# Two second products moved into an attention's opening steps, its first two normalisations moved to another engine, four output rows stored plainly

## The chip, the cores and the metric

The kernel runs on one core of a Trainium2 chip. A core has TensorE (PE, matmuls; its weight loads are listed as PEld), VectorE (DVE), ScalarE (ACT), GpSimd (POOL) and SyncE (SP, which here only issues DMAs). The metric is the device time of one execution in microseconds (us); lower is better.

## The reference

One layer of an encoder block: an input projection of the normalised stream feeds a retention branch and a windowed attention branch; both are gated, projected, mixed by sigmoid gates, projected once more, normalised, and added to x. T is 1040 (16 meta tokens and 1024 positions), the model width 1024.

```python
u = _rms_norm(h, pre_w)
z = u @ w_in
rq, rk, rv, rg, aq, ak, av, ag, gr, ga = _split_in(z)
...
o_r = o_r * ret_nw.astype(jnp.float32) * jax.nn.silu(rg.astype(jnp.float32))
y_r = o_r.astype(h.dtype) @ w_rb
...
s = jnp.concatenate([s_band, s_meta], axis=-1)
m = jnp.maximum(jnp.max(s, axis=-1, keepdims=True), sink_l)
p = jnp.exp(s - m)
p = p / (jnp.sum(p, axis=-1, keepdims=True) + jnp.exp(sink_l - m))
...
o_a = o_a * jax.nn.silu(ag.astype(jnp.float32))
y_a = o_a.astype(h.dtype) @ w_ab
mix = jax.nn.sigmoid(gr) * y_r + jax.nn.sigmoid(ga) * y_a
out = mix @ w_o
return h + _rms_norm(out, post_w)
```

## The kernel before

Every matmul is done in three parts (`mm3`, lines 94 to 96): operands are split into a high and a low part (ACT casts the high part, DVE subtracts it at line 110), and high by high, low by high and high by low are summed in PSUM. The large projections are Strassen-like block products: seven products of half-size blocks, whose operands are sums and differences of weight or stream blocks, made on DVE, and whose results DVE and ACT add into the outputs. A phase is named by a letter, and its products accumulate in tiles `by`, `bz`, `br`, `ba` and `bo`.

The program runs in this order: a setup and the retention heads (to about 335 us), the first phase with tiles `by` (gates and queries), the attention, and then the phases z (gates), r and a (the two branch projections) and o (the output projection).

*Units.* Ten output units (`LATER`, numbers 4 to 15) have three of their seven products done early, as fill between other work: their product 2 ("second products", tiles `pe4_2` to `pe15_2`) and their products 3 and 5 ("fifths", tiles `pe4_5` and so on). A unit's second product is 12 matmuls of 128 x 512, in four pieces of three. In the first phase a table, `FIRST_AT`, says at which step of the program which job is written (an engine may do it earlier or later): `m4` is four pieces of second products, `x0` and `y0.0` load and split parts of the output weight, `L4`, `S4`, `P4` and `F4` belong to the weights of unit 4 for the fifths. The names at line 854 (load `we`), 861 to 863 (its sums, on DVE) and 790 (`w5_...h`, the cast) are these steps.

*Attention.* It goes by 32 steps of 64 queries, 16 for each of two groups of heads. `stage1` makes masked scores for two tiles (`ps` on PE, `raw` with its row minimum `nm` on DVE, line 1525; the exponential `p` with its row sum on ACT, 1528; the reciprocal of the sum on DVE, 1531; p times that reciprocal on POOL, 1538, or for the last blocks of the second group on ACT, 1535). `stage2` transposes p on PE (`pt`, 1549 and 1552) and splits it, `stage3` multiplies it with the values (`po`). Between these, `fill` runs pieces of the fifths: `START` gives the numbers ahead of the first two blocks' scores, `FILL` two numbers for each later step, each in half pieces; `BEGUN` says at which piece the jobs of the fifths (loads, sums, splits) are started. A second product's piece and a fifth's piece are each three matmuls and cost two.

*Output.* `o_post` takes each finished half row block (128 rows of 512). Squares go to ACT, the mean's power to POOL, and the normalised rows are written by POOL with an accumulating DMA to `out`, where x was copied ahead during the retention heads. Row 3 alone loads x into SBUF and is finished by DVE and stored plainly by SP.

The order within each engine is that of the program, with explicit marks (`follow`) that keep DVE and ACT work behind the scores and transposes.

Of the kernel before, what the change touches and what calls it, by code (L numbers as in the profile page):

```python
# [12 lines left out]
D = 1024  # L13
# [10 lines left out]
HALVES = [(16, 528), (528, 1040)]  # L24
MW = 720
NC = 2 * NB
START = 4, 12
FILL = ((2, 2),) * 1 + ((3, 1),) * 1 + ((2, 3),) * 1 + ((2, 2),) * 1 + ((4, 3),) * 1 + ((2, 3),) * 6 + ((2, 4),) * 1 + ((2, 3),) * 1 + ((2, 4),) * 1 + ((2, 3),) * 1 + ((3, 3),) * 1 + ((2, 1),) * 1 + ((2, 2),) * 1 + ((2, 3),) * 2 + ((2, 4),) * 1 + ((0, 4),) * 1 + ((2, 2),) * 1 + ((2, 3),) * 3 + ((3, 3),) * 1 + ((2, 4),) * 1 + ((1, 3),) * 1
EARLY = 8, 9
LATER = 4, 10, 5, 11, 6, 12, 7, 13, 14, 15  # L30
PRE = {u: (2, 3, 5) for u in LATER}
BORDER = 12, 0, 12
LAST = 9
REFILL = -48, 6, 5
LATE = -15, -14, -12, -9, -7, -6, -5, -3, -3, -1

LEADS = 2, 4, 6
VALUES_AT = ((-1, "w1", "s0", "s1"), (1, "l2"), (4, "w0"), (6, "c2"), (8, "n6", "s2", "pT2.0.1.2"),
             (16, "f0", "l3"), (17, "f1", "f2"), (20, "c3", "z"), (21, "s3", "f3"), (22, "pT2.3"))
FIRST_AT = ((1, "k6"), (2, "pT3"), (6, "pT4"), (7, "m4"), (12, "tT3", "tT4"), (13, "x0"), (14, "tT2"),  # L40
# [4 lines left out]

U_QK, U_V, U_G = 0, 4, 8
# [9 lines left out]
def block_kernel(ctx: ExitStack, tc: tile.TileContext, xT, x, meta, w_in, w_rb, w_ab, w_out, vecs, dec, sink,  # L56
# [463 lines left out]
    def retention(h, fill):  # L520
# [127 lines left out]
        def finish(c):  # L648
            o = op[c - 1]
            to = (p2 if c > 2 else p1)(f"to{h}_{c}")  # L650
            for e_ in range(2):
                nc.tensor.transpose(to[:, P * e_:P * e_ + P], o[:, P * e_:P * e_ + P], ident)  # L652
            if c % 2 == 0:
                ost[0] = rp.tile([P, 2, 256], F32, tag="ost", bufs=2, name=f"ost{h}_{c}")
            w0 = P * ((c - 1) % 2)
            for e_ in range(2):
                nc.scalar.activation(ost[0][:, e_, w0:w0 + P], to[:, P * e_:P * e_ + P], AF.Copy,  # L657
                                     scale=rnw[:, 2 * h + e_:2 * h + e_ + 1])
            if c % 2 == 1:
                sent = nc.sync.dma_start(  # L660
                    oTr_d[2 * h:2 * h + 2, :, P * (c - 1):P * (c + 1)].rearrange("e p t -> p e t"), ost[0]).ins
                if h < NH - 1 and c == 5:
                    with tc.issue_after(sent):
                        r, e_ = ((0, 3), (4, 6), (6, 8))[h]
                        nc.sync.dma_start(out[P * r:P * e_], x[P * r:P * e_])

        for c in range(NB, 0, -1):
# [311 lines left out]
    def gtile(name):  # L979
        return gp.tile([P, 512], F32, tag="g", bufs=gates_[0], name=name)  # L980
# [205 lines left out]
    def refill(nm, src):  # L1186
# [38 lines left out]
        def got(n):  # L1225
            return lambda: get_pre(n)
# [34 lines left out]
            return d  # L1261
        if nm == "a":
            return {-16: [load(0, 0)], -14: [load(1, 1)], -13: [plain("B11", 0, 0)], -11: [got("T1")],
                    -10: [load(1, 0)], -9: [got("T2")], -7: [plain("B21", 1, 0)], -5: [got("T3")],
                    -3: [plain("B22", 1, 1)], -1: [got("T4")]}
        return {-16: [load(0, 0), load(0, 1)], -14: [load(1, 1)], -13: [plain("B11", 0, 0)], -11: [t1],
                -10: [load(1, 0)], -9: [t2, t3], -7: [b21], -5: [plain("T3", 0, 1)], -3: [plain("B22", 1, 1)],
# [105 lines left out]


    pw = rbc[:, 0:D]
    rows, xres = {}, []

    def o_head():
        nc.sync.dma_start(pw, post_w.partition_broadcast(P))
# [5 lines left out]
    def o_post(u, i, j, o, to=None):  # L1385
        if not rows:
            o_head()
        r = 2 * (u ^ 2) + i
        s = slice(512 * j, 512 * j + 512)
        if r not in rows:  # L1390
            rows[r] = (gp.tile([P, 3], F32, tag="ms2", bufs=4, name=f"ms2_{r}"), [], [])
            if r == 3:
                xres.append(lp.tile([P, 4, 256], F32, tag="wr", bufs=2, name="xres").rearrange("p a b -> p (a b)"))
                nc.sync.dma_start(xres[0], x[P * r:P * r + P])
        m2, parts, _ = rows[r]
        square(r, m2, j, o)
        to = o if to is None else to
        if u == 3:
            to = gtile(f"pw{r}_{j}")
            nc.vector.tensor_tensor(to, o, pw[:, s], mul)  # L1400
        parts.append((s, to, o))
        if len(parts) == 2:
            o_out(r)

    def square(r, m2, c, o):
        m1 = rows[r][2]
        jk = gtile(f"jk{r}_{c}")
        nc.scalar.activation(jk[:, 0:o.shape[1]], o, AF.Square, accum_out=m2[:, c:c + 1])
        if not m1:
            m1.append(gp.tile([P, 1], F32, tag="ms1", bufs=4, name=f"ms1_{r}"))  # L1410
            nc.vector.tensor_scalar(m1[0], m2[:, c:c + 1], 0.25 / D, EPS, op0=ALU.mult, op1=ALU.add)
        else:
            nc.vector.scalar_tensor_tensor(m1[0], m2[:, c:c + 1], 0.25 / D, m1[0], op0=ALU.mult, op1=ALU.add)

    def o_out(r):
        m2, parts, (m1,) = rows[r]
        nc.gpsimd.tensor_tensor(m1, m1, mhalf[:, 0:1], ALU.pow)
        for s, to, o in parts:
            if r == 3:
                nc.vector.scalar_tensor_tensor(to, to, m1, xres[0][:, s], op0=ALU.mult, op1=ALU.add)  # L1420
                nc.sync.dma_start(out[P * r:P * r + P, s], to)
                continue
            if r == 2:
                nc.scalar.activation(to, to, AF.Copy, scale=m1)
            else:
                nc.vector.scalar_tensor_tensor(to, o, m1, pw[:, s], op0=ALU.mult, op1=ALU.mult)
            nc.gpsimd.dma_start(out[P * r:P * r + P, s], to, accum_op=ALU.add)

    def o_tail(o, a):
        m2, parts, _ = rows[3]  # L1430
        s = slice(a, a + 256)
        square(3, m2, 2 * (a // 256), o[:, s])
        if not a:
            xres.append(gtile("pw3_0"))
        nc.vector.tensor_tensor(xres[1][:, s], o[:, s], pw[:, s], mul)
        if a:
            parts.append((slice(0, 512), xres[1], o))
            o_out(3)

    seq = [(u, p) for p in (1, 7, 5, 6, 2, 3, 4) for u in (0, 1)]  # L1440
# [49 lines left out]
    def attention():  # L1490
# [18 lines left out]
        def stage1(g, b):  # L1509
# [21 lines left out]
            last["sum"] = nc.vector.reciprocal(den, den).ins  # L1531
            softmax.append(last["sum"])
            for e_ in range(2):
                if g and b > 2 * NB - 3:
                    softmax.append(nc.scalar.activation(pt[e_][:, 0:wid], pt[e_][:, 0:wid], AF.Copy,
                                                        scale=den[:, e_:e_ + 1]).ins)
                    continue
                nc.gpsimd.tensor_scalar(pt[e_][:, 0:wid], pt[e_][:, 0:wid], den[:, e_:e_ + 1], 1.0, op0=ALU.mult,  # L1538
                                        op1=ALU.mult)
# [40 lines left out]


        chunks = [(g, b) for g in range(2) for b in range(2 * NB)]
        works = hooked([(fifths(), 2)], BEGUN)
        owed = [0]

        def fill(n):
# [142 lines left out]
    for n, _ in enumerate(first):  # L1729
# [8 lines left out]
    yp = spare[0] = at1  # L1738
    vah, val = (atv.tile([P, NB, 256], R, name=n) for n in ("vah", "val"))

    BEGUN = {5: [(pre_sums, 5), (pre_fetch, 11)],
             6: [(pre_parts, 5)],
             7: [(pre_low, 5)],
             13: [(pre_sums, 11), (pre_fetch, 6)],
             14: [(pre_parts, 11)],
             15: [(pre_low, 11)],
             21: [(pre_sums, 6), (pre_fetch, 12)],
             22: [(pre_parts, 6)],
             23: [(pre_low, 6)],
             24: [(load_k,)],  # L1750
             29: [(pre_sums, 12), (pre_fetch, 7)],
             30: [(pre_parts, 12), (pre_low, 12)],
             37: [(pre_sums, 7), (pre_fetch, 13)],
             38: [(pre_parts, 7)],
             39: [(pre_low, 7)],
             40: [(pre_load, 3, act_src(w_out))],
             45: [(pre_sums, 13), (pre_fetch, 14)],
             46: [(pre_parts, 13)],
             47: [(pre_low, 13)],
             48: [(pre_split, 3, 0)],  # L1760
             50: [(pre_split, 3, 1)],
             52: [(pre_split, 3, 2)],
             53: [(pre_sums, 14), (pre_fetch, 15)],
             54: [(pre_parts, 14), (pre_split, 3, 3)],
             55: [(pre_low, 14)],
             61: [(pre_sums, 15)],
             63: [(pre_parts, 15), (pre_low, 15)]}

    i = attention()
    next(i)  # L1770
# [112 lines left out]
```

## Time and profile before

| what | us |
|---|---|
| runs | 1049.03, 1053.14, 1053.15 (median 1053.14) |
| the profiled execution | 1051.43 |
| its span | 1049.7 |
| PE busy in the span | 1030.0 |
| DVE, ACT, POOL busy | 842.1, 511.0, 217.5 |

The profile's times are those of one execution, of which 1.7 us lie around the span. PE's busy time is that of its matmuls, which overlap: one matmul of 512 columns shows about 0.39 us and is followed by the next after about 0.23. "Waits" tell for which instruction of another engine an engine stood idle.

### The profile page before, as it was taken

How to read it: one execution, taken by the hardware profiler on the slowest of the kernel's cores; microseconds unless marked ns; L12 is line 12 of the kernel's file. 1: busy time of each engine (PE TensorE's matmuls, PEld its weight loads, DVE VectorE, ACT ScalarE, POOL GpSimd, SP SyncE). 2: the span in 40 equal slices, each digit the busy share in tenths (PEclk: the TensorE clock that was granted, in tenths of full speed). 3: DMA queues.
4: the chain of work that ended last, by engine and by line, in shares of the span. 5: the costliest groups of instructions: out<-in, count | busy, mean ns of one | idle time of the engine just before them, and what ended most of it. 6: DMA issues, size and time to landing. Idle time of an engine off the chain costs nothing.

```text
span 1049.7 us, 17233 instructions
## 1 busy us (share of the span) xinstructions
PE 1030.0 (98%) x5797; PEld 893.0 (85%) x5797; DVE 842.1 (80%) x1734; ACT 511.0 (49%) x1116; POOL 217.5 (21%) x284
## 2 busy tenths in 40 slices
PE   8999999999999999999899999999999999999997
PEld 7998999989999888888689998888888888787885
DVE  7887788779889787985878886699899799768665
ACT  5541441423435643423567777476567355343443
POOL 3424235235233002231123321000000000111042
PEclk9999999999999999999899999999999999999998
DMA  9422311315244499997866775999889648789365
GB/s 335 161 81 91 101 42 51 111 32 200 77 141 142 124 409 322 262 312 217 313 213 211 233 246 161 357 374 347 308 300 336 237 138 269 195 237 316 95 101 81
DMA packets 117577, 217.17 MB, mean 207 GB/s; under 512 B 12672, under 2 KB 44320, under 8 KB 114864
## 3 DMA queue, kind: packets, MB, share of 16 engines
q1 hardware_dynamic: 111040, 204.78, 56.9%
q0 software_dynamic: 6304, 11.01, 7.0%
q8 instruction: 46, 0.75, 0.3%
q14 instruction: 43, 0.35, 0.1%
q10 hardware_dynamic: 144, 0.27, 0.1%
HBM read 142.57 MB, written 77.12 MB: 209 GB/s over the span
## 4 chain that ended last, share of the span: by engine, by line
PE 86%; DVE 5%; DMA 5%; issue 1%; SPq 1%; ACT 1%; POOL 0%; DVEq 0%; POOLq 0%; ACTq 0%
PE bz L95 5%; PE bz L94 5%; PE bz L96 5%; PE by L95 4%; PE by L96 4%; PE by L94 4%; PE pv L95 3%; PE pv L94 3%; PE pv L96 3%; PE bo L95 3%; PE bo L94 3%; PE br L95 2%; PE bo L96 2%; PE br L94 2%; PE br L96 2%; PE ba L95 2%
## 5 line engine op out<-in xcount | busy, mean ns | idle before, releaser
L94 PE MATMUL pv<-wh,big 128*128 128x256 f32 x256 | 73.3, 286 | 0.0
L95 PE MATMUL pv<-wh,big 128*128 128x256 f32 x256 | 72.9, 285 | 0.0
L96 PE MATMUL pv<-wl,big 128*128 128x256 f32 x256 | 72.5, 283 | 0.0
L1538 POOL TENSOR_SCALAR p<-p,den 128x352 f32<-128x352 f32 (+2 forms) x60 | 38.4, 653 | 127.2 <-DVE den L1531 109.9
L1369 POOL DMA_DIRECT2D mx_d<-c1a x4 | 3.5, 875 | 287.3 <-DVE c1a L1360 287.3
L94 PE MATMUL bz<-T,lhz 128*128 128x512 f32 x144 | 56.8, 395 | 0.0
L95 PE MATMUL bz<-T,llz 128*128 128x512 f32 x144 | 56.8, 394 | 0.0
L96 PE MATMUL bz<-T,lhz 128*128 128x512 f32 x144 | 56.8, 394 | 0.0
L1012 ACT CAST why<-wry 128x512 fp32r<-128x512 f32 x56 | 33.2, 620 | 48.3 <-PE by L96 27.1
L95 PE MATMUL by<-big,wly 128*128 128x512 f32 x128 | 50.7, 396 | 0.0
L94 PE MATMUL by<-big,why 128*128 128x512 f32 x128 | 50.4, 394 | 0.0
L96 PE MATMUL by<-big,why 128*128 128x512 f32 x128 | 50.4, 394 | 0.0
L1453 POOL DMA_DIRECT2D aq_d<-m_aq x32 | 27.3, 1277 | 102.6 <-DVE u3y L1448 65.9
L95 PEld LDWEIGHTS pv<-wh,big 128*128 128x128 f32 x256 | 48.2, 188 | 0.3
L94 PEld LDWEIGHTS pv<-wh,big 128*128 128x128 f32 x256 | 48.2, 188 | 0.2
L96 PEld LDWEIGHTS pv<-wl,big 128*128 128x128 f32 x256 | 48.3, 189 | 0.2
L110 DVE TENSOR_TENSOR wly<-wry,why 128x512 fp32r<-128x512 f32 x56 | 37.9, 693 | 12.1 <-ACT why L1012 11.9
L1528 ACT ACTIVATE p<-raw,nm 128x353 f32<-128x353 f32 (+2 forms) x64 | 36.2, 567 | 18.2 <-DVE nm L1525 17.0
L595 ACT ACTIVATE op<-pa,rcol 128x256 f32<-128x256 f32 x32 | 15.3, 478 | 41.9 <-PE pa L96 41.6
L1525 DVE CUSTOM_DVE_ANT_0 raw<-ps,mask,nsink 128x352 f32<-128x352 f32 (+2 forms) x64 | 33.2, 548 | 2.7 <-ACT p L1528 1.9
L657 ACT ACTIVATE ost<-to,rnw 128x128 f32<-128x128 f32 x64 | 20.1, 366 | 31.3 <-PE to L652 21.8
L687 POOL TENSOR_TENSOR rs<-rs,mhalf 128x1 f32<-128x1 f32 x32 | 23.3, 729 | 52.1 <-DVE rs L686 48.9
(716 smaller groups left out, 3768.5 us busy)
## 6 DMA issues: line engine op xcount, KB each, us to landing
e<-e SPq DMA_DIRECT2D x60, 256.0 KB, 5.1
we<-in_w_in_dram SPq DMA_DIRECT2D x20, 512.0 KB, 5.5
wr<-in_w_in_dram SPq DMA_DIRECT2D x19, 512.0 KB, 4.0
wry<-in_w_in_dram SPq DMA_DIRECT2D x16, 512.0 KB, 7.0
tg<-tg_d SPq DMA_DIRECT2D x32, 256.0 KB, 4.7
T<-tT SPq DMA_DIRECT2D x6, 1024.0 KB, 10.4
T<-preT SPq DMA_DIRECT2D x6, 1024.0 KB, 7.3
wrz<-in_w_in_dram SPq DMA_DIRECT2D x20, 256.0 KB, 5.3
```

The costliest lines, as they stand in the source:

```text
L94: nc.tensor.matmul(o, ah, bh, start=first, stop=False, **kw)
L95: nc.tensor.matmul(o, al, bh, start=False, stop=False, **kw)
L96: latest[:] = [nc.tensor.matmul(o, ah, bl, start=False, stop=last, **kw).ins]
L110: return nc.vector.tensor_tensor(o, i, hi.bitcast(F32), ALU.subtract).ins
L595: nc.scalar.activation(o, pa[:, 0:256], AF.Copy, scale=rcol[:, c:c + 1])
L657: nc.scalar.activation(ost[0][:, e_, w0:w0 + P], to[:, P * e_:P * e_ + P], AF.Copy, scale=rnw[:, 2 * h + e_:2 * h + e_ + 1])
L687: nc.gpsimd.tensor_tensor(rs, rs, mhalf[:, 0:1], ALU.pow)
L1012: nc.scalar.copy(h, src)
L1453: nc.gpsimd.dma_start(d[a], m2[b], accum_op=ALU.add)
L1525: nc.vector.tensor_tensor_reduce(raw[e_][:, 1:1 + wid], s[:, 0:wid], mask[:, mo:mo + wid], -SCALE, nsink[:, hp:hp + 1], ALU.add, ALU.min, ...
L1528: last["exp"] = nc.scalar.activation(p[:, 0:1 + wid], raw[e_][:, 0:1 + wid], AF.Exp, scale=-1.0, bias=nm_[:, e_:e_ + 1], accum_out=den[:, ...
L1538: nc.gpsimd.tensor_scalar(pt[e_][:, 0:wid], pt[e_][:, 0:wid], den[:, e_:e_ + 1], 1.0, op0=ALU.mult, op1=ALU.mult)
```

## The change

- Of the four jobs `m4` in `FIRST_AT` two go. In PE's order the second products of units 7 and 13 stay where they were, among the first phase's early products; those of units 14 and 15, which stood among its later ones, are done in the attention ahead of the fifths (`SECONDS = 8` pieces). `START` grows from 4 and 12 to 12 and 18, `FILL` is another table, and the keys of `BEGUN` move by eight pieces. Some jobs of the two tables change places, among them the load and splits of the output weight (`x0`, `y0`).
- The p of the first two blocks of the first group is normalised by ACT rather than POOL.
- Rows 0 to 2 of the output are stored as row 3 is: x is loaded by SP into `xres`, DVE multiplies the row with the norm's weight, and then scales it and adds x; SP stores it. Row 2 has its second half finished after the next row's first sums. The copies of x into these rows of `out` go.
- In phase a's refill, the third sum's tiles (T3) are loaded after product -4 rather than -5 counted from the end of the phase.

```diff
-START = 4, 12
-FILL = ((2, 2),) * 1 + ((3, 1),) * 1 + ((2, 3),) * 1 + ((2, 2),) * 1 + ...
+START = 12, 18
+FILL = ((2, 5),) * 1 + ((3, 1),) * 1 + ((2, 3),) * 1 + ((3, 2),) * 1 + ...
+SECONDS = 8
-FIRST_AT = ((1, "k6"), (2, "pT3"), (6, "pT4"), (7, "m4"), (12, "tT3", "tT4"), (13, "x0"), (14, "tT2"),
-            (16, "y0.0"), (17, "y0.1"), (18, "y0.2"), (19, "y0.3", "x1"), (23, "y1.0"), (24, "m4", "y1.1"),
+FIRST_AT = ((1, "k6"), (2, "pT3"), (6, "pT4"), (7, "x0"), (10, "tT4", "y0.0"), (11, "y0.1"),
+            (12, "tT3", "y0.2"), (13, "y0.3"), (14, "tT2"), (19, "x1"), (23, "y1.0"), (24, "y1.1"),
...
-                if h < NH - 1 and c == 5:
+                if h in (0, 2) and c == 5:
                     with tc.issue_after(sent):
-                        r, e_ = ((0, 3), (4, 6), (6, 8))[h]
+                        r = 4 + h
+                        e_ = r + 2
                         nc.sync.dma_start(out[P * r:P * e_], x[P * r:P * e_])
...
-                    -10: [load(1, 0)], -9: [got("T2")], -7: [plain("B21", 1, 0)], -5: [got("T3")],
+                    -10: [load(1, 0)], -9: [got("T2")], -7: [plain("B21", 1, 0)], -4: [got("T3")],
...
-            if r == 3:
-                xres.append(lp.tile([P, 4, 256], F32, tag="wr", bufs=2, name="xres").rearrange("p a b -> p (a b)"))
-                nc.sync.dma_start(xres[0], x[P * r:P * r + P])
+            if r < 4:
+                pool = lp if r > 1 else keep
+                xres[r] = pool.tile([P, 4, 256], F32, tag="wr", bufs=2, name=f"xres{r}").rearrange("p a b -> p (a b)")
+                nc.sync.dma_start(xres[r], x[P * r:P * r + P])
...
-        square(r, m2, j, o)
+        if r == 3:
+            with follow(*near):
+                behind.pop()()
+        summed = square(r, m2, j, o)
         to = o if to is None else to
-        if u == 3:
+        if u > 1:
             to = gtile(f"pw{r}_{j}")
-            nc.vector.tensor_tensor(to, o, pw[:, s], mul)
+            with follow(*([summed] if r == 2 and parts else ())):
+                nc.vector.tensor_tensor(to, o, pw[:, s], mul)
...
+        def final(s, to):
+            nc.vector.scalar_tensor_tensor(to, to, m1, xres[r][:, s], op0=ALU.mult, op1=ALU.add)
+            nc.sync.dma_start(out[P * r:P * r + P, s], to)
+
+        for n, (s, to, o) in enumerate(parts):
+            if r == 2 and n:
+                behind.append(lambda s=s, to=to: final(s, to))
                 continue
-            if r == 2:
-                nc.scalar.activation(to, to, AF.Copy, scale=m1)
-            else:
-                nc.vector.scalar_tensor_tensor(to, o, m1, pw[:, s], op0=ALU.mult, op1=ALU.mult)
+            if r in xres:
+                final(s, to)
+                continue
+            nc.vector.scalar_tensor_tensor(to, o, m1, pw[:, s], op0=ALU.mult, op1=ALU.mult)
             nc.gpsimd.dma_start(out[P * r:P * r + P, s], to, accum_op=ALU.add)
...
-                if g and b > 2 * NB - 3:
+                if b > 2 * NB - 3 if g else b < 2:
                     softmax.append(nc.scalar.activation(pt[e_][:, 0:wid], pt[e_][:, 0:wid], AF.Copy,
                                                         scale=den[:, e_:e_ + 1]).ins)
                     continue
...
-        works = hooked([(fifths(), 2)], BEGUN)
+        works = hooked([(pieces(pre, SECONDS), 2), (fifths(), 2)], BEGUN)
```

On PE, ahead of the attention's first scores (`ps0_0`), stood the first six matmuls of unit 4's product 5, right behind the first phase's last product (`by3_5`). Before:

```order
L95 MATMUL by3_5_6305<-big1_0_137,wly3_3_6399 128x512
L96 MATMUL by3_5_6305<-big1_1_139,why3_3_6398 128x512
L94 MATMUL pe4_5_6621<-big0_0_136,w5_4h_6472 128x512
L95 MATMUL pe4_5_6621<-big0_0_136,w5_4l_6473 128x512
L96 MATMUL pe4_5_6621<-big0_1_138,w5_4h_6472 128x512
L94 MATMUL pe4_5_6621<-big0_0_136,w5_4h_6472 128x512
L95 MATMUL pe4_5_6621<-big0_0_136,w5_4l_6473 128x512
L96 MATMUL pe4_5_6621<-big0_1_138,w5_4h_6472 128x512
L94 MATMUL ps0_0_6630<-kTh0_6507,aqh0_0_6513 128x208
```

Now, at the same place:

```order
L95 MATMUL pe14_2_6588<-big1_0_137,w2_8h_5882 128x512
L96 MATMUL pe14_2_6588<-big1_0_137,w2_8l_5883 128x512
L97 MATMUL pe14_2_6588<-big1_1_139,w2_8h_5882 128x512
L95 MATMUL pe15_2_6604<-big1_0_137,w2_8h_5882 128x512
L96 MATMUL pe15_2_6604<-big1_0_137,w2_8l_5883 128x512
L97 MATMUL pe15_2_6604<-big1_1_139,w2_8h_5882 128x512
L95 MATMUL pe15_2_6604<-big1_0_137,w2_8h_5882 128x512
L96 MATMUL pe15_2_6604<-big1_0_137,w2_8l_5883 128x512
L97 MATMUL pe15_2_6604<-big1_1_139,w2_8h_5882 128x512
L95 MATMUL ps0_0_6613<-kTh0_6474,aqh0_0_6480 128x208
```

All 12 matmuls of unit 14 and the first six of unit 15 (line numbers are one higher) stand there now; the rest of unit 15, all 12 of `pe4_5` and 9 of `pe10_5` follow between the first and the second block's scores, where 6 of `pe4_5` and 12 of `pe10_5` stood.

On ACT, from the attention's table load on. Before, p goes from its exponentials to POOL:

```order
L886 COPY e4_5_6655<-pe4_5_6621 128x512
L886 COPY e10_5_6682<-pe10_5_6658 128x512
L1528 ACT_TABLE_LOAD
L1528 ACTIVATE p0_0_6635,den0_0_6629<-raw0_6611,nm0_0_6628 128x209
L1528 ACTIVATE p1_0_6643,den0_0_6629<-raw1_6612,nm0_0_6628 128x209
L1528 ACTIVATE p0_1_6692,den0_1_6687<-raw0_6611,nm0_1_6686 128x289
L1528 ACTIVATE p1_1_6699,den0_1_6687<-raw1_6612,nm0_1_6686 128x289
L1555 CAST pah0_0_6711<-pt1_0_0_6705 128x256
```

Now:

```order
L1538 ACT_TABLE_LOAD
L1538 ACTIVATE p0_0_6618,den0_0_6612<-raw0_6578,nm0_0_6611 128x209
L1538 ACTIVATE p1_0_6626,den0_0_6612<-raw1_6579,nm0_0_6611 128x209
L1545 ACTIVATE p0_0_6618<-p0_0_6618,den0_0_6612 128x208
L1545 ACTIVATE p1_0_6626<-p1_0_6626,den0_0_6612 128x208
L1538 ACTIVATE p0_1_6684,den0_1_6679<-raw0_6578,nm0_1_6678 128x289
L888 COPY e10_5_6720<-pe10_5_6657 128x512
L1538 ACTIVATE p1_1_6691,den0_1_6679<-raw1_6579,nm0_1_6678 128x289
L1565 CAST pah0_0_6703<-pt1_0_0_6697 128x256
L1566 CAST pbh0_0_6705<-pt2_0_0_6700 80x256
L741 CAST aqh0_2_6711<-qf0_2_6449 128x512
L792 CAST w5_5h_6675<-we5_0_6470 128x1024
```

The first block's scalings (line 1545) stand right behind its exponentials; the copy of `e10_5` moved between the second block's two exponentials, and that block's scalings stand behind the four casts shown last.

On SP, in phase a's last products, `wro` is the mix loaded for phase o and `T31` the second tile of the third sum. Before:

```order
L1347 DMA tg1_301_11482<-tg_d_69 128x512
L1351 DMA mr301_11484<-mx_d_68 128x512
L1383 DMA wro0_0_11562<-mx_d_68 128x4x256
L1174 DMA T31_8891<-preT31_124 128x2048
L1383 DMA wro1_0_11588<-mx_d_68 128x4x256
```

Now:

```order
L1349 DMA tg1_301_11481<-tg_d_69 128x512
L1353 DMA mr301_11483<-mx_d_68 128x512
L1385 DMA wro0_0_11561<-mx_d_68 128x4x256
L1385 DMA wro1_0_11585<-mx_d_68 128x4x256
L1176 DMA T31_8890<-preT31_124 128x2048
```

The second load of the mix passed the tile of T3.

More of the change, by code (lines that the diff above doesn't have):

```diff
@@ L26 @@
 NC = 2 * NB
-START = 4, 12
-FILL = ((2, 2),) * 1 + ((3, 1),) * 1 + ((2, 3),) * 1 + ((2, 2),) * 1 + ((4, 3),) * 1 + ((2, 3),) * 6 + ((2, 4),) * 1 + ((2, 3),) * 1 + ((2, 4),) * 1 + ((2, 3),) * 1 + ((3, 3),) * 1 + ((2, 1),) * 1 + ((2, 2),) * 1 + ((2, 3),) * 2 + ((2, 4),) * 1 + ((0, 4),) * 1 + ((2, 2),) * 1 + ((2, 3),) * 3 + ((3, 3),) * 1 + ((2, 4),) * 1 + ((1, 3),) * 1
+START = 12, 18
+FILL = ((2, 5),) * 1 + ((3, 1),) * 1 + ((2, 3),) * 1 + ((3, 2),) * 1 + ((4, 3),) * 1 + ((0, 2),) * 1 + ((4, 3),) * 1 + ((3, 3),) * 1 + ((2, 3),) * 2 + ((2, 2),) * 1 + ((2, 4),) * 1 + ((2, 3),) * 1 + ((2, 4),) * 1 + ((2, 3),) * 2 + ((3, 1),) * 1 + ((1, 3),) * 1 + ((2, 3),) * 2 + ((2, 4),) * 1 + ((0, 4),) * 1 + ((2, 3),) * 1 + ((2, 2),) * 1 + ((1, 3),) * 1 + ((2, 3),) * 2 + ((2, 4),) * 1 + ((1, 4),) * 1
 EARLY = 8, 9
@@ L37 @@
 LEADS = 2, 4, 6
-VALUES_AT = ((-1, "w1", "s0", "s1"), (1, "l2"), (4, "w0"), (6, "c2"), (8, "n6", "s2", "pT2.0.1.2"),
-             (16, "f0", "l3"), (17, "f1", "f2"), (20, "c3", "z"), (21, "s3", "f3"), (22, "pT2.3"))
-FIRST_AT = ((1, "k6"), (2, "pT3"), (6, "pT4"), (7, "m4"), (12, "tT3", "tT4"), (13, "x0"), (14, "tT2"),
[3 rows of a table removed]
+VALUES_AT = ((-1, "s0", "s1"), (1, "w1", "l2"), (4, "w0", "n6"), (6, "c2"), (8, "s2", "pT2.0.1.2"),
+             (16, "f0", "l3"), (17, "f1", "f2"), (19, "c3"), (20, "z"), (21, "s3", "f3"), (22, "pT2.3"))
+FIRST_AT = ((1, "k6"), (2, "pT3"), (6, "pT4"), (7, "x0"), (10, "tT4", "y0.0"), (11, "y0.1"),
[3 rows of a table added]
             (52, "L4", "F5", "A2"), (53, "S10", "P10", "A3"), (54, "m4", "L10"))
@@ L1375, in block_kernel @@
     pw = rbc[:, 0:D]
-    rows, xres = {}, []
+    rows, xres, behind = {}, {}, []
     def o_head():
@@ L1410, in square @@
             m1.append(gp.tile([P, 1], F32, tag="ms1", bufs=4, name=f"ms1_{r}"))
-            nc.vector.tensor_scalar(m1[0], m2[:, c:c + 1], 0.25 / D, EPS, op0=ALU.mult, op1=ALU.add)
-        else:
-            nc.vector.scalar_tensor_tensor(m1[0], m2[:, c:c + 1], 0.25 / D, m1[0], op0=ALU.mult, op1=ALU.add)
+            return nc.vector.tensor_scalar(m1[0], m2[:, c:c + 1], 0.25 / D, EPS, op0=ALU.mult, op1=ALU.add).ins
+        return nc.vector.scalar_tensor_tensor(m1[0], m2[:, c:c + 1], 0.25 / D, m1[0], op0=ALU.mult,
+                                               op1=ALU.add).ins
     def o_out(r):
@@ L1417, in o_out @@
         nc.gpsimd.tensor_tensor(m1, m1, mhalf[:, 0:1], ALU.pow)
[L1418 to L1421, printed above, removed]
+        def final(s, to):
[4 more added lines that the diff above has]
+                behind.append(lambda s=s, to=to: final(s, to))
                 continue
-            if r == 2:
-                nc.scalar.activation(to, to, AF.Copy, scale=m1)
-            else:
-                nc.vector.scalar_tensor_tensor(to, o, m1, pw[:, s], op0=ALU.mult, op1=ALU.mult)
+            if r in xres:
+                final(s, to)
+                continue
+            nc.vector.scalar_tensor_tensor(to, o, m1, pw[:, s], op0=ALU.mult, op1=ALU.mult)
             nc.gpsimd.dma_start(out[P * r:P * r + P, s], to, accum_op=ALU.add)
@@ L1432, in o_tail @@
         square(3, m2, 2 * (a // 256), o[:, s])
-        if not a:
-            xres.append(gtile("pw3_0"))
-        nc.vector.tensor_tensor(xres[1][:, s], o[:, s], pw[:, s], mul)
         if a:
-            parts.append((slice(0, 512), xres[1], o))
+            to = gtile("pw3_0")
+            nc.vector.tensor_tensor(to, o, pw[:, 0:512], mul)
+            parts.append((slice(0, 512), to, o))
             o_out(3)
@@ L1739, in block_kernel @@
     vah, val = (atv.tile([P, NB, 256], R, name=n) for n in ("vah", "val"))
[L1741 to L1767, printed above, removed]
+    BEGUN = {13: [(pre_sums, 5), (pre_fetch, 11)],
+             14: [(pre_parts, 5)],
+             15: [(pre_low, 5)],
+             21: [(pre_sums, 11), (pre_fetch, 6)],
+             22: [(pre_parts, 11)],
+             23: [(pre_low, 11)],
+             29: [(pre_sums, 6), (pre_fetch, 12)],
+             30: [(pre_parts, 6)],
+             31: [(pre_low, 6)],
+             32: [(load_k,)],
+             37: [(pre_sums, 12), (pre_parts, 12), (pre_fetch, 7)],
+             38: [(pre_low, 12)],
+             45: [(pre_sums, 7), (pre_fetch, 13)],
+             46: [(pre_parts, 7)],
+             47: [(pre_low, 7)],
+             48: [(pre_load, 3, act_src(w_out))],
+             53: [(pre_sums, 13), (pre_fetch, 14)],
+             54: [(pre_parts, 13)],
+             55: [(pre_low, 13)],
+             56: [(pre_split, 3, 0)],
+             58: [(pre_split, 3, 1)],
+             60: [(pre_split, 3, 2)],
+             61: [(pre_sums, 14), (pre_fetch, 15)],
+             62: [(pre_parts, 14), (pre_split, 3, 3)],
+             63: [(pre_low, 14)],
+             69: [(pre_sums, 15)],
+             71: [(pre_parts, 15), (pre_low, 15)]}
     i = attention()
```

4 rows, old and new, of the table FIRST_AT are left out of this document.

## The prediction

> **What bounds the kernel now.** I read the profile's page first, for which engine fills the span:
>
> ```profile
> span 1049.7 us, 17233 instructions
> PE 1030.0 (98%) x5797; PEld 893.0 (85%) x5797; DVE 842.1 (80%) x1734; ACT 511.0 (49%) x1116; POOL 217.5 (21%) x284
> ```
>
> TensorE (PE) is busy for 1030.0 of 1049.7 us, so 19.7 us of its idle time is all there is to win, apart from matmuls that run at a lower granted clock. The change adds no matmul and drops none. Then I read PE's waits over the whole span, and after them its busy time by stretches, to see where the idle time lies:
>
> ```profile
> PE pt L1549 <- POOL p L1538: 3.0, 2, 2.7
> PE ps L94 <- DVE nm L1525: 1.9, 1, 1.9
> PE bo L95 <- DVE llo L110: 0.6, 1, 0.6
> ...
> 450.00:475.00 25.00, 25.00 (x110) 20.28 (x109) 18.45 (x30) 6.74 (x12) 10.65 (x14) 1.00 1.06 305
> 475.00:500.00 25.00, 25.00 (x110) 20.46 (x109) 15.60 (x24) 11.59 (x21) 2.84 (x4) 1.00 0.75 205
> 500.00:525.00 25.00, 20.08 (x89) 16.16 (x88) 20.82 (x47) 13.57 (x29) 4.25 (x6) 0.86 0.88 318
> ```
>
> The columns of a stretch are its length, busy time of PE, weight loads, DVE, ACT and POOL, the granted clock, the DMA share and GB/s. One stretch, 500 to 525, holds 4.92 us of idle time and a clock of 0.86. It is the attention's opening. Finer stretches show the clock, and the timeline shows the steps:
>
> ```profile
> 516.00:518.00 2.00, 1.41 (x5) 0.94 (x6) 1.75 (x5) 0.84 (x3) 1.87 (x3) 0.50 0.99 401
> 518.00:520.00 2.00, 2.00 (x7) 1.71 (x7) 1.52 (x4) 1.90 (x4) 0.71 (x2) 0.50 0.96 320
> 520.00:522.00 2.00, 2.00 (x7) 1.69 (x6) 2.00 (x4) 0.31 (x1) 0.00 (x0) 0.50 0.98 362
> ...
> 507.66 0.39 PE L94 MATMUL pe<-big,w_10h 128*128 128x512 f32 x1
> 510.21 0.40 PE L96 MATMUL pe<-big,w_10h 128*128 128x512 f32 x1
> 512.05 0.43 DVE L1525 CUSTOM_DVE_ANT_0 raw<-ps,mask,nsink 128x208 f32<-128x208 f32 x1
> 512.54 0.40 PE L94 MATMUL ps<-kTh,aqh 128*128 128x288 f32 x1 [1.93 <-DVE nm L1525]
> 512.82 1.28 ACT L1528 ACT_TABLE_LOAD   x1
> 514.11 0.47 ACT L1528 ACTIVATE p<-raw,nm 128x209 f32<-128x209 f32 x1
> 515.15 0.17 DVE L1531 RECIPROCAL den<-den 128x2 f32<-128x2 f32 x1
> 515.43 3.28 POOL L1538 TENSOR_SCALAR p<-p,den 128x208 f32<-128x208 f32 x4 [37.58 <-DVE den L1531]
> 516.32 0.47 PE L1549 MATMUL pt<-ident,p 128*128 128x128 f32 x1 [2.72 <-POOL p L1538]
> 517.28 0.18 PEld L1549 LDWEIGHTS pt<-ident,p 128*128 128x128 f32 x1 [0.71 <-POOL p L1538]
> ```
>
> PE runs out of its fill products at 510.61, waits 1.93 us for the first masked scores (`raw`), and after 1.06 us of the next scores 2.72 us for the first normalised p, which POOL makes only after a table load, the exponential and a reciprocal. From 516 to 522 the granted clock is 0.50, with PE busy for 1.41 + 2.00 + 2.00 = 5.4 us. At full clock half of it would do, so 2.7 us go there. Idle time and clock together make about 7.6 us, the ceiling of this place.
>
> Why is `raw` so late? The chain of waits shows DVE's queue behind one load:
>
> ```profile
> 484.48 7.92 DMA we<-in_w_in_dram
> 492.43 0.69 DVE we L861
> ...
> 482.55 0.33 SPq L854 DMA_DIRECT2D we<-in_w_in_dram  x1
> 483.88 1.81 SPq L854 DMA_DIRECT2D we<-in_w_in_dram  x3
> ...
> we<-in_w_in_dram SPq DMA_DIRECT2D x20, 512.0 KB, 5.5
> ```
>
> DVE gets the weights of unit 4 at 492.43 and works through its queue almost without a gap until `raw` at 512.05: 33 operations in 19.62 us, 0.595 us each.
>
> **The change part by part.**
>
> *Second products moved.* A second product's matmul of 512 columns takes 0.232 us: 11 steps from 507.66 to 510.21. The last two second products are 24 matmuls, 5.57 us. Before, they stood among the last products of the first phase; now they are the first fill of the opening. By the order, 24 fill matmuls stood ahead of the second block's scores, now 45. PE comes to these scores 24 - 21 = 3 matmuls sooner, 510.61 - 0.70 = 509.9. This shift itself is worth nothing; what it does is to fill the time while DVE works. The sum depends on when `raw` comes. Between the load and `raw` stand 31 operations now (two gate posts go ahead of the load's wait), 31 x 0.595 = 18.4 us. The second half of the load is issued after a store, at about 483.9. With 5.5 us to landing (the page's median) `raw` starts at 483.9 + 5.5 + 18.4 = 507.8; with the 7.92 us of this load's own row at 510.2. DMA share there is 0.75, below the 1.06 ahead of it, and one 256 KB store fewer stands among the loads, so I take the lower half, `raw` at 508.5; both ends stay for the range.
>
> *Normalising of the first two blocks on ACT instead of POOL.* The price is in the kernel already, for the last two blocks:
>
> ```profile
> 648.01 0.97 ACT L1535 ACTIVATE p<-p,den 128x288 f32<-128x288 f32 x2
> L1528 ACT ACT_TABLE_LOAD x1 | 1.3, 1283 | 0.0
> ```
>
> That is 0.49 us each, against 3.28 / 4 = 0.82 us on POOL, and in the second row, the groups of 500 to 655 us, the attention has one table load for exponentials and these scalings together, so none is added. From `raw` to the first normalised p it took 516.32 - 512.05 = 4.27 us; now 515.15 + 0.17 - 512.05 = 3.27, plus about 0.5, is 3.8. PE, after 1.06 us of scores, is at the transposes at 509.9 + 1.06 = 511.0; p is there at 508.5 + 3.8 = 512.3. The wait is 1.3 us, where 1.93 + 2.72 stood. The second transpose pair waits 0.1 to 0.3 us. What is queued behind the new ACT work: the scaling of block 1 stands behind two casts, a query split and a weight cast in ACT's queue, and the second exponential behind a copy for which PE must first have done its transposes. I work block 1's p out to be about 1.0 us later than PE's fill lasts (0 to 1.5). Idle time after: 1.3 + 0.2 + 1.0 = 2.5. With no wait over 1.5 us I take the clock to stay. Gain 7.6 - 2.5 = 5.1 us; ends: 7.6 - 1.8 = 5.8 for `raw` at 507.8, and for `raw` at 510.2 idle time of 0.8 ahead of the scores and 2.2 + 0.3 + 1.0 behind them, 4.3, and perhaps the clock again: 3.3, or 0.6 with 2.7 off.
>
> The Trainium skill, "ScalarE: Activation LUTs", section "What ACT_TABLE_LOAD costs", gives 2.66 us for a switch of tables, of which some 1.38 us is a drain. The rows above disagree: 1.28 us at 512.82 and the exponential at 514.11, at once behind it; by the page p would come 1.4 us later, and the gain would be 3.7.
>
> *The first phase.* What did these 24 matmuls cover there? The tightest of the last splits:
>
> ```profile
> 481.10 0.69 DVE L110 TENSOR_TENSOR wly<-wry,why 128x512 fp32r<-128x512 f32 x1 [1.92 <-ACT why L1012]
> 487.83 0.39 PE L95 MATMUL by<-big,wly 128*128 128x512 f32 x1
> ```
>
> The last block of (3,2) is split at 481.79 and first multiplied at 487.83, 6.04 us later. Should the split stay where it was, 6.04 - 5.57 = 0.47 us of cover are left; where it waits for a buffer that PE frees, it moves along. So I cost it at nothing. If the cover is gone, PE waits by as much as a load is late beyond that. Moved w_out loads and splits (from hooks 13 and 16 to 19 to hooks 7 and 10 to 13) pass other loads in SP's queue and other splits in DVE's earlier, but all in the first half of the phase's hooks (which run to 54).
>
> *Third sums loaded behind the mix.* SP now issues the second o block's mix load ahead of the second T3 tile. The 0.6 us that `bo` waits for `llo` may go: between 0 and 0.65 us, I take 0.4.
>
> *Output rows.* Six accumulating stores leave POOL, six plain ones come to SP, three 512 KB loads of x come, and 1.5 MB of copies of x leave the retention heads, where PE doesn't wait for SP. DVE gets four multiplications and two more finals that ACT did; ACT loses two. The rows that end the kernel:
>
> ```profile
> 1040.81 1.79 POOL L1427 DMA_DIRECT2D out_dram<-pw  x2 [1.12 <-ACT pw L1424]
> 1043.91 1.42 DVE L1420 SCALAR_TENSOR_TENSOR pw<-pw,ms,xres 128x512 f32<-128x512 f32 x2 [0.75 <-POOL ms L1417]
> 1044.69 1.00 SPq L1421 DMA_DIRECT2D out_dram<-pw  x2
> 1025.00:1050.00 25.00, 16.91 (x85) 14.05 (x83) 12.41 (x26) 7.31 (x19) 7.65 (x10) 0.89 0.54 85
> ```
>
> The last chain (DVE, then SP's stores) is that of row 3, which stays. Six more DVE operations of about 0.7 us are 4.2 us; DVE is idle for 12.6 of the last 25 us, so I cost them at 0.2. If all fell on the last chain they would cost 4; without POOL's stores beside the last ones it could gain 0.5.
>
> **Sum.** 5.1 + 0.4 - 0.2 = 5.3 us; 1051.43 - 5.3 = 1046.1 for the profiled execution (span 1049.7 and 1.7 around it), which lies 1.7 below the median of the runs, 1053.14, and 2.4 above the lowest; I forecast 1046.
>
> **Rivals.**
>
> *A: as worked out*, 1045.4 (gain 5.8 + 0.2) to 1047.9 (3.3 + 0.2) by the ends of `raw`, the clock kept; 0.62.
>
> *B: the load lands no sooner, and the clock falls again.* For it: the load took 7.92 us here, four loads of 512 KB are still issued together, and PE would be idle for 0.8 and 2.2 us around 1 us of work. Against it: in the trace the clock fell after 1.93 + 2.72 us of idle time around 1 us of work. Gain 0.6, less 0.2, plus 0.4: 0.8, 1050.6; where `raw` comes only at 511, 1051.4. Chance 0.23. The Trainium skill, "TensorE: Matmul & The Clock Gate", section "What's actually happening", has the clock halved after an idle window of about 3.4 us in a free-running count; the trace agrees in the size of the step (0.50), and whether 2.2 us would do isn't shown here.
>
> *C, slower: the loads of the first phase come late.* DMA share is 1.06 from 450 to 475, and SP's queue is rearranged there. A load of 512 KB at 305 GB/s takes 1.7 us; two more ahead of the last `wry` loads make them 3.4 late, and past 0.47 us of cover PE waits 3.0 us. The load of unit 4, behind them, is 3.4 late as well, at 492.43 + 3.4 + 18.4 = 514.2 `raw` starts, and PE, at 512.9, waits 1.8 for the scores and then 2.2 + 0.3 + 1.0, with 2.7 for the clock: 8.0. If the wait in the first phase costs a drop of the clock too (2.7), the loss is 3.0 + 2.7 + 8.0 - 7.6 = 6.1 us, 1057.5. It decides from loads about 0.5 us later than before. Against it: covers elsewhere are longer and no load is added in the second half of the phase. Chance 0.15.
>
> **How the numbers follow.** About 0.5% (5.3 us) is what a measurement of this kernel can tell from no change. A's middle lies just there; with an earlier landing or the tail's and the mix's best on top, some two thirds of A are beyond it: 0.40 faster. The rest of A and B: 0.45 the same. C: 0.15 slower. The likeliest is A, 1046. The range leaves out C but for its beginning and takes in the ends of A with the tail's and the mix's best (1051.43 - 7.6 - 0.65 - 0.5 = 1042.7) and B with half of the tail's worst: 1051.4 + 2 = 1053.4.
>
> **What would show it.** Right: no gap of PE before the second block's scores, one of 1 to 1.5 us before the first transpose, granted clock 1.00 from 510 to 525, first `raw` near 508.5, no gap of PE between 340 and 500, and the chain's end still DVE's finals of row 3. Wrong: `raw` past 510 or a clock of 0.50 (B), a wait of `by` for `wly` or `why` (C), a wait of `bo` in the last 40 us, or a last chain that goes through other rows than row 3.

## The result: slower, by 0.6%

The changed kernel takes 1058.01 us (median of 6 runs, 1056.08 to 1059.44) against 1052.01 (6 runs, 1049.03 to 1053.15). The ratio is 1.0056, with a 95% interval from 1.0040 to 1.0072. The forecast was 1046, and its range ended at 1053.4. The page of the changed kernel, four of PE's longest waits, and the busy time in three stretches around the opening:

```profile
span 1054.3 us, 17250 instructions
PE 1030.5 (98%) x5797; PEld 893.2 (85%) x5797; DVE 842.0 (80%) x1739; ACT 510.9 (48%) x1118; POOL 207.6 (20%) x274
...
PE by L95 <- ACT u2y L1108: 4.9, 1, 4.9
PE pt L1559 <- DVE pal L111: 4.1, 2, 3.9
...
PE pt L1559 <- ACT p L1545: 1.5, 2, 0.9
PE pe L95 <- ACT e L888: 1.4, 1, 1.4
...
475.00:500.00 25.00, 20.10 (x81) 16.30 (x81) 13.08 (x21) 10.19 (x20) 3.44 (x5) 0.93 0.74 188
500.00:525.00 25.00, 22.18 (x105) 17.45 (x104) 21.67 (x47) 15.76 (x34) 0.00 (x0) 1.00 0.93 317
525.00:550.00 25.00, 21.09 (x122) 18.80 (x121) 14.53 (x40) 13.35 (x36) 5.87 (x10) 0.93 0.70 218
```

The opening (500 to 525) is better, as meant: 22.18 us busy where it was 20.08, and the clock stays at 1.00. But the stretch ahead of it, which had no idle time, now has 4.9 us, and the stretch behind it 3.9, both with a clock of 0.93.

Where the time goes is seen best from one PE instruction that both kernels have to the next. The table has the us between them, from the traces, one execution each: from the first phase's first product (`by0_1`) to the end of its last (`by3_5`), on to the end of the fourth block's scores (`ps0_3`), to the end of the attention's last transpose of a full 128 x 128 tile, to PE's last matmul, and to the span's end. The move takes 5.57 us of matmuls from the first column to the second; so "moved" gives before's times with just that.

| kernel | first phase | opening | attention | phases z to o | tail |
|---|---|---|---|---|---|
| before | 167.59 | 20.42 | 127.79 | 389.33 | 7.75 |
| before, work moved | 162.02 | 25.99 | 127.79 | 389.33 | 7.75 |
| after | 168.80 | 21.78 | 133.23 | 388.56 | 6.85 |
| copies of 7 and 13 early | 162.00 | 25.29 | 134.49 | 389.51 | 6.84 |
| the same, unit 11 apart | 162.07 | 24.15 | 131.38 | 389.66 | 6.84 |
| all units two ahead | 162.37 | 25.88 | 129.69 | 389.14 | 6.86 |
| move undone | 167.59 | 19.03 | 130.78 | 389.75 | 6.84 |

Against the second row the changed kernel loses 6.8 us in the first phase and 5.4 in the attention, and wins 4.2 in the opening, 0.8 in the phases z to o and 0.9 at the tail. The first loss is no accident of one execution: in the five other traces whose first phase is the changed kernel's (all edits of it further down that keep its job table) the phase takes 167.8 to 170.5 us, with the same wait of 3.7 to 5.7. The second is less sure, as "The move undone" will show. (What comes ahead of `by0_1` scatters from 335.1 to 338.4 between these profiles.)

The first loss on the timeline of the changed kernel, ACT, POOL, SP and PE, and the clock behind it:

```profile
466.99 0.97 SPq L1461 DMA_DIRECT2D aq_d<-c5y  x2
473.33 5.11 POOL L1463 DMA_DIRECT2D aq_d<-m_aq  x6 [6.18 <-DMA aq_d<-c5y]
477.82 0.59 ACT L888 COPY e<-pe 128x512 f32<-128x512 f32 x1 [10.42 <-DMA aq_d<-m_aq]
479.34 0.59 ACT L1108 COPY u2y<-by 128x512 f32<-128x512 f32 x1
479.98 0.80 PE L95 MATMUL by<-T3q,why 128*128 128x512 f32 x1 [4.90 <-ACT u2y L1108]
480.00:482.00 2.00, 2.00 (x5) 1.62 (x6) 0.25 (x1) 0.00 (x0) 0.00 (x0) 0.50 0.95 251
482.00:484.00 2.00, 2.00 (x8) 1.59 (x7) 0.18 (x1) 1.32 (x3) 0.00 (x0) 0.67 0.42 100
```

Read the first five rows from the last up: PE waits for a PSUM bank (`by`) that ACT must empty (copy `u2y`). ACT stood 10.42 us in its queue ahead of that, at the copy of unit 7's second product (`e`), because the copy's buffer still held an `m_aq` whose accumulating DMA hadn't landed. And POOL stood idle for 6.18 us ahead of these DMAs, until SP's plain store to the same rows (`aq_d<-c5y`) had landed, 5.8 us after its issue. The same hold stood in before's trace, at nearly the same time, with unit 14's copy in that place (the first row is from the list of those who waited for `m_aq`, since the timeline names no releaser for this copy):

```profile
  ACT e L886: 5.7, 1
...
476.75 0.59 ACT L886 COPY e<-pe 128x512 f32<-128x512 f32 x1 [5.68 <-issue]
478.28 0.59 ACT L1106 COPY u2y<-by 128x512 f32<-128x512 f32 x1
480.25 0.39 PE L95 MATMUL pe<-big,w_8l 128*128 128x512 f32 x1
482.12 0.39 PE L94 MATMUL by<-T3q,why 128*128 128x512 f32 x1
```

There PE did second products until 482.12, by when the bank had been free for 3.25 us (from 478.87). Take 5.57 us of cover away, and the hold comes 2.3 us into the open. The rest of the 4.9 is that the copy `u2y` also came later: at 144.25 us from `by0_1` (479.34 - 335.09) rather than 141.50 (478.28 - 336.78), 2.75 us. The two make 5.1; PE's products stood in a slightly other order. Why the hold lasted longer in the changed kernel wasn't tested.

The wait of unit 4's load, the opening and the attention's stall, in the changed kernel:

```profile
489.92 1.53 SPq L856 DMA_DIRECT2D we<-in_w_in_dram  x2
495.97 0.69 DVE L863 TENSOR_TENSOR we<-we,we 128x512 f32<-128x512 f32 x1 [2.89 <-DMA we<-in_w_in_dram]
514.38 0.43 DVE L1535 CUSTOM_DVE_ANT_0 raw<-ps,mask,nsink 128x208 f32<-128x208 f32 x1
518.28 0.33 PE L1559 MATMUL pt<-ident,p 128*128 128x128 f32 x1 [0.86 <-ACT p L1545]
531.45 0.92 SPq L856 DMA_DIRECT2D we<-in_w_in_dram  x2
538.48 0.69 DVE L863 TENSOR_TENSOR we<-we,we 128x512 f32<-128x512 f32 x1 [5.16 <-DMA we<-in_w_in_dram]
540.65 0.82 PE L1559 MATMUL pt<-ident,p 128*128 128x128 f32 x4 [3.91 <-DVE pal L111]
```

`raw` starts 18.41 us after the load's arrival, for which the prediction had 18.4, by its 31 operations. Only the load arrives at 495.97 rather than 490, since its second half is issued 6 us later (489.92), behind the store of a gate post whose product PE had delayed by its wait. In the attention DVE stands 5.16 us at unit 11's load, and the split that PE needs (`pal`) is queued behind it; SP issues that load at 531.45, where before it was issued at 526.47 and 528.30.

### The profile page after: what moved, and what is told of

It reads as the page before. It is cut to its first block, busy times and chain, and to the rows that moved or that the text cites. A ratio compares the mean times of both kernels' runs of the same rounds, so it can differ in the third digit from the quotient of the medians.

```text
span 1054.3 us, 17250 instructions
## 1 busy us (share of the span) xinstructions
PE 1030.5 (98%) x5797; PEld 893.2 (85%) x5797; DVE 842.0 (80%) x1739; ACT 510.9 (48%) x1118; POOL 207.6 (20%) x274
## 5 line engine op out<-in xcount | busy, mean ns | idle before, releaser
L1548 POOL TENSOR_SCALAR p<-p,den 128x352 f32<-128x352 f32 (+2 forms) x56 | 33.7, 614 | 137.7 <-DVE den L1541 73.3
```

## The experiments

Three theories are tested (their letters are not those of the prediction's rivals): A, one root, ACT's hold in the first phase, from which the late load of unit 4 and that of unit 11 follow; B, two separate causes, the hold and the late load of unit 11; C, the prediction's slower rival, loads that come late in the first phase. Times are medians, ratios those to the kernel before, with their 95% intervals; the runs of one kernel scatter by 3 to 10 us, so that the verdicts on single steps rest on the traces, of one execution each.

**Copies of units 7 and 13 early.** The changed kernel with this edit:

```diff
-(7, "x0") ... (24, "y1.1") ... (47, "m4"), (49, "r", ...) ... (54, "m4", "L10")
+(7, "m4", "x0") ... (24, "m4", "y1.1") ... (49, "r", ...) ... (54, "L10")
```

> The changed kernel with the two remaining second-product jobs written at steps 7 and 24 of the first phase instead of 47 and 54. PE's order stays; what moves is ACT's copies of units 7 and 13 out of PSUM (and their stores), from late in the phase to early. Theory A (one root: ACT's queue is held by the copy of unit 7, whose buffer is held by an accumulating DMA; the late load of unit 4 and the late load of unit 11 in the attention follow from it): PE's 4.9 us wait for a bank near 480 goes, first raw 4 to 6 us sooner, the 3.9 us wait for pal near 540 shrinks to under 1.5, total 1058 - 10 to 12 = 1046 to 1048. Theory B (two separate causes): only the 4.9 us and its clock drop go, the wait near 540 stays over 3 us, 1051 to 1052. Theory C (the phase is held by its loads): PE still waits 3 us or more before 500, 1056 to 1058.

Measured: 1053.63 us, ratio 1.0018 (1.0000 to 1.0036), 4.4 us below the changed kernel.

```profile
PE pt L1559 <- DVE pal L111: 4.8, 3, 4.4
PE pe L95 <- ACT e L888: 3.6, 1, 3.6
...
483.24 2.11 SPq L856 DMA_DIRECT2D we<-in_w_in_dram  x2
493.33 0.69 DVE L863 TENSOR_TENSOR we<-we,we 128x512 f32<-128x512 f32 x1 [7.00 <-DMA we<-in_w_in_dram]
511.75 0.43 DVE L1535 CUSTOM_DVE_ANT_0 raw<-ps,mask,nsink 128x208 f32<-128x208 f32 x1
512.00:520.00 8.00, 8.00 (x36) 6.83 (x35) 4.77 (x16) 6.82 (x18) 0.00 (x0) 0.79 1.00 377
```

The wait for the bank is gone and the first phase takes 162.00 us, before's time less the moved work. No load of the first phase was changed; so C falls, and that ACT's queue was held at these copies is shown by experiment (what held the copy, the accumulating DMA and the store, is read from the trace). But the attention's stall stays at 4.4 us: A falls too. And the opening gains only 0.7 us on before: the load of unit 4, issued as early as in before, landed at 493.33 (492.43 before), `raw` came at 511.75, and PE now stood 3.6 us at a bank of its own fill products, whose copies lie on ACT behind gate activations that wait for DVE. The clock fell once more. So the opening gained what the prediction's rival B had for it (0.6 us), by another wait: B has PE wait for `raw` and for p, and here it waits for a bank. The two traces below that also have the copies early and that the table lists show the same (3.5 and 3.7 us); no run moved the copies of the fill, so that how much more the move could gain stays open.

**Unit 11's sums later.** Keys 21, 22, 23 of `BEGUN` become 23, 24, 25 in the changed kernel.

> The changed kernel with unit 11's sums, cast and low part started two pieces later (23, 24, 25), so that DVE splits the fourth block's transposed p ahead of the sums that wait for unit 11's load. Theory A and B alike: the wait of pt for pal (3.9 us) goes or falls under 1 us; the fifth of unit 11 waits for its weights instead, 1 to 2.5 us, since they land no sooner; the first phase's 4.9 us wait stays. Total 1055 to 1057. If DVE's order was not the holder, the wait for pal stays at 3 to 4 us and the time at 1058.

Measured: 1057.73 us, 1.0067 (1.0048 to 1.0086), just above what was expected. The wait for `pal` went, and two waits for unit 11's weights came, 2.6 and 1.3 us:

```profile
PE pe L95 <- ACT w_11h L792: 2.6, 1, 2.6
...
PE pe L96 <- DVE w_11l L111: 1.3, 1, 1.3
```

DVE's order says who waits, the load says how long.

**Unit 11's weights in other buffers**, with the copies early (first) and in the changed kernel as it is (second):

```diff
-        pool = lp if u == LATER[1] else keep
+        pool = lp if u in LATER[1:4:2] else keep
```

> The kernel with the copies of units 7 and 13 early (the run before this), and unit 11's weights loaded into the two buffers that unit 10's had rather than those of unit 5. SP then issues unit 11's load near 508 to 512 us, ahead of the two loads of values behind which it stood, rather than near 530. Theory B (the attention's stall is a cause of its own, the late load of unit 11): the 4.4 us wait of pt for pal near 540 goes, with its clock drop, and 5 to 6 us of time: 1048 to 1049. If DVE's or ACT's order, not the load, held that step, the wait stays over 3 us and the time at 1053 to 1054. A rival: the earlier load slows the others beside it (DMA share 1.0 from 512 to 520), and first raw or the values come 1 to 2 us later: 1050 to 1051.

> The changed kernel with nothing but unit 11's weights loaded into unit 10's buffers. Theory B: the first phase's 4.9 us wait stays, the 3.9 us wait for pal goes with its clock drop: 1058 - 5 to 6 = 1052 to 1053. If the two stalls are one (theory A), the wait for pal stays, 1057 to 1058.

Measured: 1053.82 us, 1.0008 (0.9987 to 1.0030); and 1056.28, 1.0031 (1.0011 to 1.0051). SP had issued unit 11's load by 509.66 in the first, and neither profile has a wait for `pal` of over 0.2 us any more. B holds for that step: the wait went with the first-phase wait left in place, too. But the time hardly followed. Each version was expected to win 5 to 6 us. By the ratios the first won 1.0 us and the second 2.6, with intervals that overlap those of the kernels without the edit; in the traces the attention got 3.1 us shorter in the first and 0.5 in the second (132.8). Other waits had come in its place, for the next unit's weights and the scores behind them (in the first):

```profile
554.11 0.50 PE L96 MATMUL pe<-big,w_6l 128*128 128x512 f32 x1 [1.46 <-DVE w_6l L111]
562.55 0.43 PE L95 MATMUL ps<-kTh,aqh 128*128 128x352 f32 x1 [1.20 <-DVE nm L1535]
564.00:566.00 2.00, 2.00 (x7) 1.71 (x6) 1.97 (x6) 2.00 (x6) 0.83 (x2) 0.50 0.69 212
```

**All units two ahead.** With the copies early, all units of the fifths use the two pairs of buffers in turn (`LATER[1::2]`), with their fetches earlier in `BEGUN` (6 at 16, 12 at 24, 7 at 32, 13 at 39, 14 at 48, 15 at 56), and unit 6's sums two pieces earlier; then also unit 14's sums four pieces earlier and 15's two.

> The kernel with units 7 and 13 early and unit 11 in unit 10's buffers, carried on: all the fifths' units take the two pairs of buffers in turn, each unit's load is started as soon as the unit two before it has left its pair (keys 16, 24, 32, 39, 48, 56 instead of 21, 29, 37, 45, 53, 61), and unit 6's sums, cast and low part two pieces earlier. If late loads and sums of the units are what is left in the attention, the waits at 552 and 561 us (1.5, 1.2 and 0.4 us, with a clock drop) go, the attention from the fourth scores on takes about 128 us as before the change, rather than 131, and the total falls by 3 to 4 from 1053.8 (the run before): 1049 to 1051, 0.1 to 0.3% below the kernel before. If DVE's own order is the limit, the waits only move on, 1053 to 1054.

> The run before (all fifths' units in two pairs of buffers in turn) with unit 14's sums, cast and low part four pieces earlier (57, 58, 59) and unit 15's two (67, 69). There PE waited 0.8 and 1.6 us near 610 for unit 14's weights, which DVE made late by its own order (the load had landed). If that is the last such wait, the gaps near 610 go, nothing over 0.5 us stands between 525 and 650, and the profile's time falls by 2.3 to 3: about 1049 against 1051.5 for the kernel before, a ratio of 0.997 to 0.999. If the wait moves on to unit 15 or to the transposes, 1051.5 to 1052.5.

Measured: 1052.55 us, 1.0012 (0.9996 to 1.0027); and 1052.69, 1.0010 (0.9997 to 1.0022). In the first the waits near 552 and 561 were gone, and two of 0.8 and 1.6 us for unit 14's weights stood near 610; in the second they were one of 3.3 us at 607. The attention took 129.7 and 133.0 us where 127.8 stood before. The wait moved on each time, and none of these versions beats the kernel before.

**The move undone**, all else kept (`START`, `FILL`, `VALUES_AT`, `FIRST_AT`, `BEGUN` and `works` as before).

> The changed kernel with the move undone: second products, fill tables, job tables and the pieces' jobs as before; the other three parts stay (first two normalisations on ACT, output rows, third sums behind the mix). If the move alone makes the loss, PE has no wait over 1 us before 500, about 4 us of waits in the opening, and the end is 1 to 1.3 us shorter: 1049 to 1051, the same as before or up to 0.2% faster. If another part carries a loss, it stays above 1053.

Measured: 1051.46 us, 0.9995 (0.9978 to 1.0012). No wait over 1 us between 330 and 500; the loss is the move's. The three other parts together can't be told from no change. Their trace has a wait for `pal` of 2.6 us, with a drop of the clock, where before's had 1.2. DVE stood 4.24 us at unit 11's sums in it, and 3.63 in before's trace (last two rows; the profile puts the end of both down to a load of queries issued beside unit 11's):

```profile
PE pt L1559 <- DVE pal L111: 2.7, 2, 2.6
PE pt L1559 <- ACT p L1545: 2.7, 1, 2.7
PE ps L95 <- DVE nm L1535: 2.2, 1, 2.2
...
534.00:536.00 2.00, 0.17 (x1) 0.20 (x2) 1.97 (x5) 0.00 (x0) 0.00 (x0) 0.95 0.63 183
536.00:538.00 2.00, 2.00 (x9) 1.75 (x8) 1.90 (x7) 1.35 (x2) 0.00 (x0) 0.50 0.78 271
...
533.67 0.69 DVE L863 TENSOR_TENSOR we<-we,we 128x512 f32<-128x512 f32 x1 [4.24 <-DMA qf<-aq_d]
534.24 0.69 DVE L861 TENSOR_TENSOR we<-we,we 128x512 f32<-128x512 f32 x1 [3.63 <-DMA qf<-aq_d]
```

So DVE's stall at unit 11's sums is older than the move. The attention took 130.78 us here, 3.0 over before: of the 5.4 us that the changed kernel loses there, only 2.4 are over a kernel without the move. Whether the 3.0 are the other parts' or the scatter of one execution wasn't tested.

**The other parts undone one by one**, in the changed kernel: the first blocks' p on POOL again, the output rows as before, the T3 tile ahead of the mix again.

> The changed kernel with p of the first two blocks normalised by POOL again. By the prediction's step ACT takes 0.42 us each against 0.82 on POOL, and stands behind casts for the second block: the first transpose comes 0.4 to 0.8 us later, the second 0.3 to 1 us sooner. Total within 1 us of the changed kernel, 1057 to 1059. A rival that blames ACT's longer queue for the loss expects 2 us or more less, 1056 or below.

> The changed kernel with output rows 0 to 2 stored as before (accumulating DMAs on POOL, x copied ahead). From the last matmul's add to the end the changed kernel took 6.0 us against 7.3 before. If plain stores are the reason, this one takes 7 to 7.5 us there and the total rises by 1 to 1.5, 1059 to 1059.5. If they cost time by DVE's six more operations, it falls by 1 or more. PE's waits before 1000 us stay as in the changed kernel.

> The changed kernel with the second T3 tile issued ahead of the second mix load again. The prediction took the first wait of bo (0.65 us before the change) to go with the new order, and it is 0.56 us in the changed kernel. If the order matters little, bo waits 0.4 to 1.1 us here too, with the time within the runs' scatter, 1056 to 1059; if the new order did help, the wait is over 1.2 us.

Measured: 1057.60 us, 1.0062 (1.0034 to 1.0091); 1058.98, 1.0071 (1.0049 to 1.0093); and one run of 1058.31. On POOL the two waits for the first p are 1.3 and 0.5 us, on ACT 0.9 and 0.6: about 0.3 us apart. With the old rows PE's last matmul is followed by 7.67 us, with the new ones by 6.85; that is the one gain that every trace shows, 0.8 us (6.8 to 6.9 in all ten with the new rows), and too small for the medians. `bo` waited 0.7 us with the old order of the mix and 0.6 with the new (1.1 with the copies early): no gain to be seen.

## Why the prediction was wrong

- *The opening's mechanism*: right in part. In the changed kernel the clock stayed at 1.00, the first transpose came 3.9 us after `raw` (3.8 forecast) and waited 0.9 us (1.3), the next block's 0.6 (1.0). But "no gap of PE before the second block's scores" failed: PE stood 1.4 us there, and 3.6 with the copies early, at a bank of the fill itself. Its copies stand on ACT behind gate activations that wait for the same DVE work as `raw`. The prediction priced the fill's matmuls and not the banks that they fill.
- *When `raw` comes*: the chain of 31 operations was right (18.41 us), its start was wrong. I took the load to land at about 490. It came at 496.0 behind the new stall (6.05 us after its late issue), and without that stall at 493.3, 10.1 us after the issue at 483.24: there the 7.92 us of its own row was nearer than 5.5, but still short. The prediction's B was right that the load would land no sooner. The 4.2 us that the opening won in the changed kernel are thus waiting time that had been spent ahead of it.
- *"The first phase ... So I cost it at nothing"* is the step that failed. I measured the cover that the second products gave by the splits of the weights (0.47 us left). The resource that ran out was a PSUM bank, which ACT empties, and ACT's queue was held by a buffer, an accumulating DMA and a store. Its row stood in the trace of before: ACT idle for 5.68 us ahead of a copy in the middle of a phase in which PE never waits. The term was put at nothing and measured 6.8 us, 4.9 of them idle.
- *Rival C* had the place and the sign, but not the cause. That its size (6.1) is that of the loss is luck: it is 5.7 for the first phase, the clock there included, and 0.4 net in the opening, where the traces have 6.8, a gain of 4.2, and the attention's loss, which C doesn't have.
- *The attention behind the opening* was costed at nothing without a word. The changed kernel's trace lost 5.4 us there against before, 2.4 against the kernel with the move undone. That unit 11's late load, passed on by DVE's order to the transposes, made its largest wait is shown (other buffers, later sums). That the eight pieces ahead of the fifths made it late is argued from the tables: the jobs of the fifths are tied to pieces of fill, and pieces in front move each unit's load against the steps that need it.
- *Tail and third sums*: the tail gained 0.9 us instead of losing 0.2; the 0.4 for `bo` didn't come.

## What to carry to other kernels

Before fill work is taken from a stretch without idle time, list what PE takes there beside its weights, accumulation banks above all, and follow each back through the in-order queue of the engine that frees it: the longest idle time of that engine in the stretch, whatever ended it, may be what the fill covers. The fill takes its need of a bank along to where it goes. Where loads are started by counts of fill pieces, adding pieces in front moves every later load against the steps that need it. And a wait that starts at a load wasn't shortened here by giving the waiting engine other work first (3.9 us before, 2.6 and 1.3 after); it went when the load was issued sooner, though other waits then took most of its place.

## What the runs showed of the hardware

PE's clock fell to 0.50 after idle times much shorter than the 4.9 us of the first phase: after one of 2.56 us (the move undone, from 533.27), and after 1.20 and 0.36 us that stood 0.75 us of work apart (unit 11 apart, from 561.35). It didn't fall after 0.77 and 1.56 us (all units two ahead, 609 to 612) or after the 1.4, 0.9 and 0.6 of the changed kernel's opening. The Trainium skill, "TensorE: Matmul & The Clock Gate", section "What's actually happening", has the drop after an idle window of about 3.4 us that runs freely; these drops come after less. So if the window is that long, it need not be idle throughout; the runs show neither its length nor how much idle time it takes, only that the smaller sum (1.56 us) brought a drop and a larger one (2.33) did not.
